# Two instead of three ordinary feature pairs at the head of the second FFN, with token sums and first blocks written out in their order of use

## The chip, the cores and the metric

The kernel runs on one core of one Trainium2 chip. The metric is the device time of one execution in microseconds. The core has a matrix engine (TensorE, PE), a vector engine (VectorE, DVE), a scalar engine (ScalarE, ACT), GpSimd (POOL) and SyncE (SP). Here SyncE issues the plain loads and GpSimd the loads that add to what already lies in on-chip memory.

## The reference

One layer of an encoder on 512 tokens of width 1024, in float32: a half-step SwiGLU FFN, a token-mixing part (two kinds of attention, gated and projected), and a second half-step SwiGLU FFN. Each part stands between two RMS norms.

```python
def _swiglu(x, w_gate, w_up, w_down):
    return (jax.nn.silu(x @ w_gate) * (x @ w_up)) @ w_down
...
f = _swiglu(_rmsnorm(x, ffn2_pre_g[l]), ffn2_w_gate[l], ffn2_w_up[l], ffn2_w_down[l])
x = x + 0.5 * _rmsnorm(f, ffn2_post_g[l])
```

The FFN's inner width is 2816, which the kernel cuts into 22 features of 128. For each feature there is a gate piece and an up piece of weights, each 1024 x 128, stored as 128 partitions x 1024. Gate and up of one feature are called a pair.

## The kernel before

**Precision.** A float32 operand is split in two parts: a rounded one (`hi`, made by ScalarE in line 110) and the remainder (`lo`, made by VectorE in line 111, which must wait for `hi`). Each product of a weight block and tokens is three matmuls, `hi*hi`, `hi*lo` and `lo*hi` (`mm3`, lines 189 to 191).

**Ordinary pairs.** `pair` (line 207) computes one feature the plain way: for gate and for up, eight blocks of 128 rows times 512 tokens, 2 x 8 x 3 = 48 matmuls of 512 columns. The first two pairs of an FFN are made by `first_pairs` (line 216) in two token halves of 256, since the normalised tokens of the second half come later: four projections on the first half, then, after `mid(0)`, four on the second half. After the first two of these pair 0 is finished by `use` and `mid(1)` runs, after the other two pair 1 and `mid(2)`. The first four weight pieces of the second FFN were prepared earlier by DMA (`by_dma`); `fetch` converts two more pieces, if `state["stop"]` still allows it.

**Seven products.** `seven` (line 343) computes a pair with seven instead of eight block products: gate and up on the one side, the two halves of the 1024 rows on the other, and two token halves of 256. It needs sums of weight blocks and sums of token blocks. A pair has the weight blocks 1 to 7: 1 and 2 are the halves of the gate piece (tile `raw`, which has two buffers), 3 is half of the up piece (`w11`), 5 and 7 (`t1`, `t3`) are loaded by SyncE and completed by a load that adds, issued by GpSimd (`load_blocks`, line 319). 6 is 5 + 3 and 4 is 6 + 2, added by VectorE in `sums_of` (line 332), both when block 1 of the pair is made ready. Each block is split into one tile of the tag `w`, which has 12 buffers. The token blocks 1, 2 and 4 are the normalised tokens themselves; 5, 6, 3 and 7 are sums made once for an FFN by the generator `combined` (line 290): its first step adds `hi` and `lo` of the first token half (four additions, line 304), each further step makes one sum (two additions, line 294) and splits it (two splits).

In the loop of `seven`, a turn j multiplies blocks 1, 5, 2, 6 and 3 of pair j and blocks 7 and 4 of pair j-1. Between them the blocks of pair j+1 are made ready, one behind each product, and the loads of pair j+2 are asked for at the top. Each product is 4 x 3 = 12 matmuls of 256 columns, 84 for a pair.

**Order of the work.** The token sums are drawn by `mid` (line 531): two steps in `mid(0)`, two in `mid(1)`, one in `mid(2)`. `STD` (line 35) is 3: three ordinary pairs, the third by `pair` in line 541, then the loop for the other 19 features. Between two marks the instructions of TensorE, ScalarE and VectorE are pinned to the order in which they are written (line 1484). For the second FFN such a stretch ends with `mid(2)`. Behind it, and on SyncE's and GpSimd's queues, a planner in the compiler orders the instructions by what it takes to be ready, with the written order as priority, and it may also put later work between pinned instructions.

The hidden features are kept in an order, `order_of` (line 1539), that the down projection wants. `times` (line 493) multiplies a feature into its place; for the features that ordinary pairs make it keeps the product aside and, once its neighbour is there, GpSimd copies it in (line 508).

Of the kernel before, what the change touches and what calls it, by code (L numbers as in the profile page):

```python
# [16 lines left out]
ALU = mybir.AluOpType  # L17
# [7 lines left out]
NF = 2816 // P  # L25
# [6 lines left out]
SPREAD = 4  # L32
URGENT = 400
FIRST = (4, 5, 6, 7)
STD = 3
BLOCKS = (10, 10)
BYDMA = (2, 3, 4)
AHEAD = 6
WARM = (0, 1, 0, 1, 9, 2)
PINNED = (mybir.EngineType.PE, mybir.EngineType.Activation, mybir.EngineType.DVE)  # L40

# [2 lines left out]
def block_kernel(ctx, tc, x, gains, weights, rpb_near, rpb_all, alibi0, alibi12, out):  # L44
    nc = tc.nc
# [12 lines left out]
    def unit(dt=F32, name="u"):  # L58
        return up.tile([P, 512], dt, tag="u", name=name)
# [49 lines left out]
    def split(hi, lo, src):  # L109
        nc.scalar.copy(hi, src)  # L110
        nc.vector.tensor_tensor(lo, src, hi.bitcast(F32), op=ALU.subtract)  # L111
# [1 line left out]

    pieces = {}
    loads = deque()
    state = {"used": False, "next": 0, "take": 0, "stop": 2 * STD, "ahead": lambda: None}
    ordered = []
    pool = []
    total = weights.shape[0]
# [199 lines left out]
    def load_blocks(n):  # L319


        r = wp.tile([P, PIECE], F32, tag="raw", name="raw", bufs=2)
        w11, t1, t3 = unit(name="w11"), unit(name="t1"), unit(name="t3")
        nc.sync.dma_start(t1, weights[n + 1][:, :512])
        nc.sync.dma_start(t3, weights[n + 1][:, :512])
        nc.sync.dma_start(r, weights[n])
        nc.sync.dma_start(w11, weights[n + 1][:, 512:])
        nc.gpsimd.dma_start(t1, weights[n][:, :512], accum_op=ALU.add)  # L328
        nc.gpsimd.dma_start(t3, weights[n + 1][:, 512:], accum_op=ALU.add)
        return {1: r[:, :512], 2: r[:, 512:], 3: w11, 5: t1, 7: t3}  # L330

    def sums_of(raw):
        t2, t4 = unit(name="t2"), unit(name="t4")
        nc.vector.tensor_tensor(t2, raw[5], raw[3], op=ALU.add)  # L334
        nc.vector.tensor_tensor(t4, t2, raw[2], op=ALU.add)
        raw[6], raw[4] = t2, t4

    def split_block(raw):
        w = wp.tile([P, PIECE], F32R, tag="w", name="w")
        split(w[:, :512], w[:, 512:], raw)  # L340
        return w

    def seven(use, mv, n_pairs, n0, behind, far, lead, raws):

        blocks = {}
        o = {}  # L350

        def get(j):
            if j < n_pairs and j not in raws:
                raws[j] = load_blocks(n0 + 2 * j)
            elif j >= n_pairs:
                behind(far)

        def ready(j, i):
            if j < n_pairs:
                if j and loads:  # L360
                    loads.popleft()()
                if i == 1:
                    sums_of(raws[j])
                blocks[j, i] = split_block(raws[j].pop(i))
            else:
                behind(lead)

        def product(j, i, key, start):
            if start:
                o[key, j] = bank(key)  # L370
            w = blocks.pop((j, i))
            acc = o[key, j][:, :256]
            for k in range(4):
                mm3(acc, w[:, k * P:(k + 1) * P], w[:, 512 + k * P:512 + (k + 1) * P], *mv[i][k],
                    start and k == 0, k == 3, skip_group_check=True)
            return acc

        res = {}
        get(0)
        get(1)  # L380
        for i in (1, 5, 2, 6, 3, 7, 4):
            ready(0, i)
        for j in range(n_pairs + 1):
            now, was = j < n_pairs, j > 0
            get(j + 2)
            if now:
                q = product(j, 1, "q", True)
                g, u = res[j] = unit(name="g"), unit(name="up")
                nc.scalar.copy(g[:, :256], q)
            ready(j + 1, 1)  # L390
            if was:
                q0 = product(j - 1, 7, "q", False)
                g0, u0 = res.pop(j - 1)
                nc.vector.tensor_tensor(u0[:, 256:], u0[:, 256:], q0, op=ALU.subtract)
            ready(j + 1, 5)
            if now:
                p = product(j, 5, "p", True)
                nc.scalar.copy(u[:, 256:], p)
            ready(j + 1, 2)
            if now:  # L400
                r = product(j, 2, "r", True)
                nc.vector.tensor_tensor(g[:, :256], g[:, :256], r, op=ALU.add)
            ready(j + 1, 6)
            if now:
                product(j, 6, "q", False)
                nc.scalar.copy(u[:, :256], q)
            ready(j + 1, 3)
            if was:
                product(j - 1, 4, "q", False)
                use(j - 1, g0, u0, q0)  # L410
            ready(j + 1, 7)
            if now:
                product(j, 3, "p", False)
                nc.vector.tensor_tensor(u[:, :256], p, u[:, :256], op=ALU.subtract)
            ready(j + 1, 4)
# [69 lines left out]
    def ffn(g, store, src):  # L485
        hidden = [None] * NF
        m = BLOCKS[store]
        feats = order_of(m)
        duos = [[None] * m for _ in range(2)]
        parts = {}  # L490
        n0 = state["take"]

        def times(j, a, b):

            k = feats.index(j)
            if k >= 2 * m or j < STD:
                hidden[k] = b
                nc.vector.tensor_tensor(b, a, b, op=ALU.mult)
                return
            to = lambda i, k: duos[i][k // 2][:, (k % 2) * 256:(k % 2) * 256 + 256]  # L500
            parts = [slice(i * 256, i * 256 + 256) for i in range(2)]
            for i, part in enumerate(parts):
                if duos[i][k // 2] is None:
                    duos[i][k // 2] = unit(name="h")
                nc.vector.tensor_tensor(to(i, k), a[:, part], b[:, part], op=ALU.mult)
            if k % 2 and hidden[k - 1] is not None:
                for i, part in enumerate(parts):
                    nc.gpsimd.tensor_copy(to(i, k - 1), hidden[k - 1][:, part])
                hidden[k - 1] = None

        def stat(k):
            if k not in parts:
                parts[k] = unit(F32R), unit(F32R)
                split(*parts[k], hidden[k])
                hidden[k] = None
            return parts[k]

        def use(j, pg, pu):
            h = unit(name="h")
            nc.scalar.activation(h, pg, AF.Silu)  # L520
            times(j, pu, h)

        def use7(j, g, u, q):
            nc.scalar.activation(g[:, :256], g[:, :256], AF.Silu)
            nc.scalar.activation(g[:, 256:], q, AF.Silu)
            times(STD + j, u, g)

        raws = {}
        sums = combined()

        def mid(i):
            if i == 0:
                for j in range(2):
                    raws[j] = load_blocks(n0 + 2 * STD + 2 * j)
            for _ in range((2, 2, 1)[i]):
                next(sums)

        first_pairs(use, (0, 2) if store else (1, 2), mid=mid)
        g_post, g_pre = gain(g), None if store else gain(g + 1)
        for j in range(2, STD):  # L540
            pair(use, j)
        if not store:
            bias_plan()
        after = n0 + 2 * NF
        state["stop"] = total if store else total - 3 * NF - NK

        far, lead, rest = down(m, after, duos, stat, g_post, g_pre, store, src)
        state["next"] = state["take"] = after + 2 * m
        seven(use7, next(sums), NF - STD, n0 + 2 * STD, lambda q: [f() for f in q.popleft()], far, lead, raws)
        rest()  # L550

    def views(raw):
# [127 lines left out]
    def down(m, n0, duos, stat, g_post, g_pre, store, src):  # L680
# [66 lines left out]
        def add_later(i, of, key, wait=0):  # L747
            for d in range(nd):
                later.setdefault(order.index((i, d)) - AHEAD + wait, []).append(ld((key, d), *of(d)))

# [337 lines left out]
    def mixing(g):  # L1088
# [119 lines left out]
        far = [v_far(1), v_far(2)]  # L1208
# [33 lines left out]
        n0 = total - 3 * NF - NK  # L1242
# [3 lines left out]
        sums = []  # L1246
# [31 lines left out]
        ready = []  # L1278
# [15 lines left out]
        for f in range(8):  # L1294
            ya, yb = bank(), bank()
            for k in range(10):
                i, c = divmod((f * 10 + k) * P, PIECE)
# [27 lines left out]
                    rooms.append(o.duo_room("ra", f - 5) if f < 7 else o.duo_room("rb", 0))  # L1325
                    nc.sync.dma_start(rooms[-1], weights[n0 + f])
        state["take"] = state["next"] = n0 + 8
        state["stop"] = total - 3 * NF + 2 * STD

        whole[:] = [[unit(name="whole") for _ in range(2)] for _ in range(2)]  # L1330
        early = [by_dma(n) for n in first_of_next()] * 2
# [48 lines left out]
    raws = []  # L1380
# [5 lines left out]
    for n in range(2, 4):  # L1386
        raw = wp.tile([P, PIECE], F32, tag="raw", name="raw", bufs=2)
# [150 lines left out]

def order_of(m):

    lo = min(STD, NF - 2 * m)
    return [*range(lo, lo + 2 * m), *range(lo), *range(lo + 2 * m, NF)]


# [60 lines left out]
```

## Time and profile before

| | us |
|---|---|
| median of three runs | 1090.49 |
| lowest and highest run | 1090.48, 1091.98 |
| profiled execution | 1090.01 |
| its span | 1088.2 |
| TensorE busy in the span | 1078.8 |
| VectorE busy | 819.7 |
| ScalarE busy | 649.3 |
| GpSimd busy | 177.9 |

Times in the profile's rows count from the start of the span, which is a little shorter than the execution's own time. The second FFN's first projections begin at about 747 us, its seven-product loop at 783.8, its down projection at about 982. Matmuls overlap: a matmul of 256 columns is shown as 0.28 us long, though the next one starts 0.12 us later, so the distance of the starts is what counts. The same holds for VectorE and ScalarE in a queue, where an operation starts before the one ahead of it has fully ended.

### The profile page before, as it was taken

The page shows a single profiled execution, that of the slowest core. Times are in us where ns is not written, and L with a number is a line of the kernel's source. Part 1 is how long each engine was busy: PE and PEld are TensorE (multiplying, and loading weights), DVE is VectorE, ACT ScalarE, POOL GpSimd, SP SyncE. Part 2 cuts the span into 40 slices and gives each one's busy share as a digit, 9 for nine tenths or more (in the row PEclk, how much of TensorE's full clock was granted, in tenths as well). Part 3 has the DMA queues.
Part 4 walks back from the last instruction along what each step waited for, and adds up shares of the span by engine and source line. Part 5 has one row for each costly group of instructions (what it writes and reads, how often), then busy time and mean ns, then how long its engine had stood idle before and what let it go on. Part 6 is the DMA issues. An engine that isn't in the chain of part 4 may idle for free. (4 is left out here: it accounts for less than half of the span.)

```text
span 1088.2 us, 18567 instructions
## 1 busy us (share of the span) xinstructions
PE 1078.8 (99%) x6821; PEld 977.7 (90%) x6821; DVE 819.7 (75%) x1514; ACT 649.3 (60%) x1300; POOL 177.9 (16%) x248
## 2 busy tenths in 40 slices
PE   9999999999999999999999999999999999999997
PEld 7999999998888988888988888888999999998886
DVE  7887777777987679876467654766897777779974
ACT  6555555565584767767656651375565555566662
POOL 3121122012334000000000001133131111114101
PEclk9999999999999999999999999999999999999999
DMA  6899898468994453332232239564577776769932
GB/s 215 223 200 241 217 244 207 138 164 252 233 296 101 126 183 119 135 90 79 66 104 78 78 118 300 162 116 140 140 188 206 196 170 182 200 174 248 237 139 77
DMA packets 90973, 184.59 MB, mean 170 GB/s; under 512 B 23553, under 2 KB 26113, under 8 KB 90882
## 3 DMA queue, kind: packets, MB, share of 16 engines
q1 hardware_dynamic: 64720, 131.03, 35.8%
q0 software_dynamic: 23472, 51.91, 26.8%
q8 instruction: 53, 0.87, 0.3%
q10 hardware_dynamic: 2690, 0.46, 0.2%
q14 instruction: 38, 0.31, 0.1%
HBM read 178.34 MB, written 7.58 MB: 171 GB/s over the span
## 5 line engine op out<-in xcount | busy, mean ns | idle before, releaser
L111 DVE TENSOR_TENSOR w<-raw,w 128x512 fp32r<-128x512 f32 (+1 forms) x139 | 129.3, 931 | 87.6 <-ACT w L110 87.0
L189 PE MATMUL ps<-hn,w 128*128 128x512 f32 (+1 forms) x488 | 174.9, 358 | 0.0
L110 ACT CAST w<-raw 128x512 fp32r<-128x512 f32 (+1 forms) x139 | 113.5, 819 | 102.5 <-DMA raw<-in_weights_dram 41.5
L191 PE MATMUL ps<-hn,w 128*128 128x512 f32 (+1 forms) x488 | 172.4, 353 | 0.0
L190 PE MATMUL ps<-hn,w 128*128 128x512 f32 (+1 forms) x488 | 172.3, 353 | 0.0
L110 ACT CAST w<-t 128x512 fp32r<-128x512 f32 x152 | 93.5, 619 | 52.0 <-DVE t L334 27.9
L111 DVE TENSOR_TENSOR w<-t,w 128x512 fp32r<-128x512 f32 x152 | 103.9, 688 | 27.1 <-ACT w L110 24.4
L191 PEld LDWEIGHTS ps<-hn,w 128*128 128x128 f32 x488 | 92.3, 189 | 12.9
L190 PEld LDWEIGHTS ps<-hn,w 128*128 128x128 f32 x488 | 92.4, 189 | 11.3
L189 PEld LDWEIGHTS ps<-hn,w 128*128 128x128 f32 x488 | 92.4, 189 | 11.3
L189 PE MATMUL q<-v,w 128*128 128x256 f32 x304 | 86.0, 283 | 0.0
L191 PE MATMUL q<-hn,w 128*128 128x256 f32 x304 | 86.0, 283 | 0.0
L189 PE MATMUL p<-v,w 128*128 128x256 f32 x304 | 86.0, 283 | 0.0
L190 PE MATMUL p<-v,w 128*128 128x256 f32 x304 | 86.0, 283 | 0.0
L191 PE MATMUL q<-v,w 128*128 128x256 f32 x304 | 86.0, 283 | 0.0
L190 PE MATMUL q<-v,w 128*128 128x256 f32 x304 | 86.0, 283 | 0.0
L190 PE MATMUL q<-hn,w 128*128 128x256 f32 x304 | 86.0, 283 | 0.0
L189 PE MATMUL q<-hn,w 128*128 128x256 f32 x304 | 86.0, 283 | 0.0
L191 PE MATMUL p<-v,w 128*128 128x256 f32 x304 | 85.9, 283 | 0.0
L328 POOL DMA_DIRECT2D t<-in_weights_dram x38 | 33.3, 877 | 289.5 <-DMA t<-in_weights_dram 67.3
L189 PE MATMUL q<-w,a 128*128 128x512 f32 x176 | 68.5, 390 | 0.0
L190 PE MATMUL q<-w,a 128*128 128x512 f32 x176 | 68.3, 389 | 0.0
(260 smaller groups left out, 2992.6 us busy)
## 6 DMA issues: line engine op xcount, KB each, us to landing
raw<-in_weights_dram SPq DMA_DIRECT2D x103, 512.0 KB
t<-in_weights_dram SPq DMA_DIRECT2D x76, 256.0 KB
t<-in_weights_dram POOLq DMA_DIRECT2D x76, 256.0 KB, 5.3
w<-in_weights_dram SPq DMA_DIRECT2D x38, 256.0 KB
w<-in_weights_dram POOLq DMA_DIRECT2D x36, 256.0 KB, 6.3
rows<-in_weights_dram SPq DMA_DIRECT2D x24, 256.0 KB
tb<-in_weights_dram POOLq DMA_DIRECT2D x12, 512.0 KB, 7.9
x<-in_x_dram SPq DMA_DIRECT2D x16, 256.0 KB
```

The lines of the kernel that those rows point to most:

```text
L110: nc.scalar.copy(hi, src)
L111: nc.vector.tensor_tensor(lo, src, hi.bitcast(F32), op=ALU.subtract)
L189: nc.tensor.matmul(o, sh, mh, start=start, stop=False, **kw)
L190: nc.tensor.matmul(o, sh, ml, start=False, stop=False, **kw)
L191: nc.tensor.matmul(o, sl, mh, start=False, stop=stop, **kw)
L328: nc.gpsimd.dma_start(t1, weights[n][:, :512], accum_op=ALU.add)
```

## The change

In the second FFN alone, `STD` becomes 2: there is no third ordinary pair, and the loop computes 20 features instead of 19. `state["stop"]` follows, so that `fetch` in `first_pairs` converts nothing there. The first FFN keeps three pairs and its order.

The three calls of `mid` now draw the token sums and split the first weight blocks in a written order, `ORDER`. `mid(0)` draws the sums of the halves and then follows its entry, `mid(1)` and `mid(2)` theirs. A `"v"` is the next token sum (5, 6, 3, 7 in turn), a tuple (j, i) is block i of pair j. These instructions lie in the pinned stretch. The sum for block 6 is made just ahead of block 6 and the sum for block 4 just ahead of block 3, in the later pairs too, where the first FFN goes on making both ahead of block 1. The first turn multiplies in the order 1, 2, 5, 6, 3 instead of 1, 5, 2, 6, 3, and block 4 of pair 0 is split after product 6 of that turn.

```diff
-STD = 3
+STD = (3, 2)
...
+ORDER = ("v", (0, 1), (0, 2)), ("v", (0, 5), (0, 6)), ("v", (0, 3), (1, 1), "v", (0, 7))
...
-    def sums_of(raw):
-        t2, t4 = unit(name="t2"), unit(name="t4")
-        nc.vector.tensor_tensor(t2, raw[5], raw[3], op=ALU.add)
-        nc.vector.tensor_tensor(t4, t2, raw[2], op=ALU.add)
-        raw[6], raw[4] = t2, t4
-
-    def split_block(raw):
+    def sum_of(raw, n):
+
+        if n not in raw:
+            raw[n] = unit(name="sum")
+            nc.vector.tensor_tensor(raw[n], *((raw[5], raw[3]) if n == 6 else (raw[6], raw[2])), op=ALU.add)
+
+    def split_block(raw, i):
+        if i in (6, 3):
+            sum_of(raw, {6: 6, 3: 4}[i])
         w = wp.tile([P, PIECE], F32R, tag="w", name="w")
-        split(w[:, :512], w[:, 512:], raw)
+        split(w[:, :512], w[:, 512:], raw[i])
         return w
...
-                if i == 1:
-                    sums_of(raws[j])
-                blocks[j, i] = split_block(raws[j].pop(i))
+                if i == 1 and not early:
+                    sum_of(raws[j], 6)
+                    sum_of(raws[j], 4)
+                if (j, i) not in blocks:
+                    blocks[j, i] = split_block(raws[j], i)
...
-        for i in (1, 5, 2, 6, 3, 7, 4):
+        for i in (1, 2, 5, 6, 3, 7) if early else (1, 5, 2, 6, 3, 7, 4):
             ready(0, i)
+
+        def fifth():
+            p = product(j, 5, "p", True)
+            nc.scalar.copy(u[:, 256:], p)
+            return p
...
-            if now:
-                p = product(j, 5, "p", True)
-                nc.scalar.copy(u[:, 256:], p)
+            if now and (was or not early):
+                p = fifth()
...
             ready(j + 1, 6)
+            if early and not was:
+                p = fifth()
             if now:
                 product(j, 6, "q", False)
                 nc.scalar.copy(u[:, :256], q)
+            if early and not was:
+                ready(0, 4)
...
         def mid(i):
+
             if i == 0:
                 for j in range(2):
-                    raws[j] = load_blocks(n0 + 2 * STD + 2 * j)
-            for _ in range((2, 2, 1)[i]):
+                    raws[j] = load_blocks(n0 + 2 * std + 2 * j)
+            if std > 2:
+                for _ in range((2, 2, 1)[i]):
+                    next(sums)
+                return
+            if i == 0:
                 next(sums)
+            for step in ORDER[i]:
+                if step == "v":
+                    next(sums)
+                else:
+                    blocks[step] = split_block(raws[step[0]], step[1])
...
-        for j in range(2, STD):
+        for j in range(2, std):
             pair(use, j)
...
-        state["stop"] = total - 3 * NF + 2 * STD
+        state["stop"] = total - 3 * NF + 2 * STD[1]
```

More of the change, by code (lines that the diff above doesn't have):

```diff
@@ L115, in block_kernel @@
     loads = deque()
-    state = {"used": False, "next": 0, "take": 0, "stop": 2 * STD, "ahead": lambda: None}
+    state = {"used": False, "next": 0, "take": 0, "stop": 2 * STD[0], "ahead": lambda: None}
     ordered = []
@@ L330, in load_blocks, with seven @@
         return {1: r[:, :512], 2: r[:, 512:], 3: w11, 5: t1, 7: t3}
-    def sums_of(raw):
-        t2, t4 = unit(name="t2"), unit(name="t4")
-        nc.vector.tensor_tensor(t2, raw[5], raw[3], op=ALU.add)
-        nc.vector.tensor_tensor(t4, t2, raw[2], op=ALU.add)
-        raw[6], raw[4] = t2, t4
-    def split_block(raw):
+    def sum_of(raw, n):
[5 more added lines that the diff above has]
+            sum_of(raw, {6: 6, 3: 4}[i])
         w = wp.tile([P, PIECE], F32R, tag="w", name="w")
-        split(w[:, :512], w[:, 512:], raw)
+        split(w[:, :512], w[:, 512:], raw[i])
         return w
-    def seven(use, mv, n_pairs, n0, behind, far, lead, raws):
-        blocks = {}
+    def seven(use, mv, n_pairs, n0, behind, far, lead, raws, blocks):
+        early = bool(blocks)
         o = {}
@@ L370, in product @@
                 o[key, j] = bank(key)
-            w = blocks.pop((j, i))
+            w = blocks[j, i]
             acc = o[key, j][:, :256]
@@ L495, in times @@
             k = feats.index(j)
-            if k >= 2 * m or j < STD:
+            if k >= 2 * m or j < STD[store]:
                 hidden[k] = b
@@ L525, in use7 @@
             nc.scalar.activation(g[:, 256:], q, AF.Silu)
-            times(STD + j, u, g)
-        raws = {}
+            times(STD[store] + j, u, g)
+        raws, blocks = {}, {}
         sums = combined()
+        std = STD[store]
         def mid(i):
@@ L548, in ffn @@
         state["next"] = state["take"] = after + 2 * m
-        seven(use7, next(sums), NF - STD, n0 + 2 * STD, lambda q: [f() for f in q.popleft()], far, lead, raws)
+        seven(use7, next(sums), NF - std, n0 + 2 * std, lambda q: [f() for f in q.popleft()], far, lead, raws, blocks)
         rest()
@@ L1539, in order_of @@
 def order_of(m):
-    lo = min(STD, NF - 2 * m)
+    lo = min(STD[1], NF - 2 * m)
     return [*range(lo, lo + 2 * m), *range(lo), *range(lo + 2 * m, NF)]
```

## The prediction

> **What bounds the kernel now.** I read the page's first part and its chain of waits first: how much of the span is TensorE, and whether anything else stands on the path.
>
> ```profile
> span 1088.2 us, 18567 instructions
> PE 1078.8 (99%) x6821; PEld 977.7 (90%) x6821; DVE 819.7 (75%) x1514; ACT 649.3 (60%) x1300; POOL 177.9 (16%) x248
> ...
> PE 31%; ACT 0%; DVE 0%; POOL 0%; issue 0%; DVEq 0%; POOLq 0%; ACTq 0%
> ```
>
> The chain is TensorE alone, so only two things can move the end: fewer TensorE microseconds, or a new TensorE wait. Next I cut the stage of the change into its steps with the view of windows (columns: stretch, length, busy time and count of PE, PEld, DVE, ACT, POOL, then clock, DMA share, GB/s).
>
> ```profile
> 761.35:772.88 11.53, 11.53 (x98) 11.53 (x97) 7.97 (x12) 4.65 (x8) 1.57 (x2) 1.00 0.91 225
> 772.88:783.79 10.91, 10.91 (x50) 9.02 (x49) 9.68 (x16) 6.71 (x11) 1.75 (x2) 1.00 0.30 48
> 783.79:793.87 10.08, 10.08 (x85) 10.07 (x84) 10.04 (x18) 8.87 (x20) 2.18 (x3) 1.00 0.62 180
> 793.87:803.95 10.08, 10.08 (x86) 10.08 (x86) 10.08 (x20) 5.41 (x13) 4.40 (x4) 1.00 0.78 213
> 870.24:880.32 10.08, 10.08 (x86) 10.08 (x85) 7.72 (x15) 5.75 (x12) 1.76 (x2) 1.00 0.73 181
> 1000.00:1040.00 40.00, 40.00 (x178) 33.12 (x177) 39.03 (x55) 27.55 (x41) 11.64 (x14) 1.00 1.06 249
> ```
>
> The rows are: the second token half of the first two pairs, the third ordinary pair, the first and second period of the seven-product loop, one of its later periods, and a stretch of the down projection. TensorE is full in every one. VectorE is full too in the first two periods of the loop (10.04 and 10.08 of 10.08), and only later falls to 7.72. So VectorE, which prepares what the loop multiplies, is the engine that has no room where the change cuts.
>
> **Part 1: the third pair becomes a twentieth turn of the loop.** The edges of that pair in TensorE's timeline:
>
> ```profile
> 772.76 0.28 PE L191 MATMUL ps<-hn,w 128*128 128x256 f32 x1
> 772.88 0.40 PE L189 MATMUL ps<-hn,w 128*128 128x512 f32 x1
> ...
> 783.57 0.39 PE L191 MATMUL ps<-hn,w 128*128 128x512 f32 x1
> 783.79 0.28 PE L189 MATMUL q<-hn,w 128*128 128x256 f32 x1
> ```
>
> It is 2 projections x 8 blocks x 3 = 48 matmuls of 512 columns from 772.88 to 783.79, 10.91 us or 0.227 each. A loop turn is 7 products x 4 blocks x 3 = 84 matmuls of 256 columns in 10.08 us, 0.120 each. The exchange saves 10.91 - 10.08 = **0.83 us**, and this is all that TensorE can gain: no row shows it waiting elsewhere in the stage. The Trainium skill speaks against the exchange: "TensorE: Matmul & The Clock Gate", section Back-to-back issue gap, gives a sustained spacing in streams of weight load and matmul of about 81 ns at 128 columns and 131 ns at 512. By it, 48 wide ones would take an estimated 6.3 us and 84 of 256 columns no less than 6.8, and the exchange would lose at least 0.5 us. The trace disagrees: this stage's spacing is 227 and 120 ns, so I go by the rows.
>
> **Part 2: what VectorE and ScalarE do at the head.** The cover that goes is the 10.91 us of the third pair: the loop's first product moves from 783.79 to 772.88. VectorE's rows of before, from the last norm on:
>
> ```profile
> 758.88 1.29 DVE L281 TENSOR_TENSOR hn<-ps,hn 128x512 fp32r<-128x512 f32 x2 [1.99 <-ACT hn L280]
> 762.52 2.36 DVE L111 TENSOR_TENSOR w<-raw,w 128x1024 fp32r<-128x1024 f32 x2 [2.35 <-ACT w L110]
> 764.80 2.49 DVE L304 TENSOR_TENSOR sum<-hn 128x512 f32<-128x512 f32 x4
> 767.20 1.29 DVE L294 TENSOR_TENSOR sum<-whole 128x512 f32<-128x512 f32 x2
> ...
> 771.57 0.69 DVE L111 TENSOR_TENSOR w<-raw,w 128x512 fp32r<-128x512 f32 x1 [2.31 <-ACT w L110]
> ...
> 775.04 0.69 DVE L498 TENSOR_TENSOR h<-ps,h 128x512 f32<-128x512 f32 x1 [0.97 <-ACT h L520]
> ...
> 778.23 1.29 DVE L294 TENSOR_TENSOR sum<-sum 128x512 f32<-128x512 f32 x2
> 779.61 1.29 DVE L111 TENSOR_TENSOR v<-sum,v 128x512 fp32r<-128x512 f32 x2
> 780.82 0.68 DVE L498 TENSOR_TENSOR h<-ps,h 128x512 f32<-128x512 f32 x1
> ```
>
> and ScalarE's:
>
> ```profile
> 759.75 1.80 ACT L288 COPY whole<-ps 128x256 f32<-128x256 f32 x6
> 761.33 2.09 ACT L110 CAST w<-raw 128x1024 fp32r<-128x1024 f32 x2
> ...
> 770.92 0.62 ACT L110 CAST w<-raw 128x512 fp32r<-128x512 f32 x1 [2.38 <-DMA raw<-in_weights_dram]
> 771.45 0.62 ACT L110 CAST w<-t 128x512 fp32r<-128x512 f32 x1
> ...
> 773.12 1.28 ACT L520 ACT_TABLE_LOAD   x1
> 774.41 0.60 ACT L520 ACTIVATE h<-ps 128x512 f32<-128x512 f32 x1
> ```
>
> Prices on VectorE: a 512-wide add costs 0.60 in a queue (2.40 for four, 764.80 to 767.20) and its result is there after 0.69; a step of token sums with its two splits 2.59 (778.23 to 780.82, a short wait for ScalarE in it); a block's split 0.60. A block that needs its sum first costs 0.69 + 0.62 (ScalarE's rounding) + 0.60, with the hand-overs 2.0. ScalarE is paced 0.53 (770.92 to 771.45) and has room.
>
> What goes from VectorE: the two 1024-wide splits of the third pair's weights (762.52 to 764.80) with the 2.35 us of idling ahead of them, and one multiplication. What is pinned in instead: blocks 1, 2, 5, 6, 3, 7 of pair 0 and block 1 of pair 1, between the sums. I queue them by these prices from 758.88 + 1.29 = 760.17: the four sums of halves end at 762.6; sums 5 at 765.2 (what they read is there at 759.75 + 1.80 = 761.55); blocks 1 and 2 at 766.4; the first pair's multiplication must wait for the second projection's end (761.35 + 48 x 0.12 = 767.1) and ends at 768.1; sums 6 at 770.7; block 5 at 771.3; block 6 at 773.3; the second multiplication at 773.9; sums 3 at 776.5; the sum for block 4 and block 3 at 777.8; block (1,1) at 778.4; sums 7 at 781.0; block 7 at 781.6.
>
> TensorE wants a product every 12 x 0.12 = 1.44 us from 772.88: product 1 at 772.9, 2 at 774.3, 5 at 775.8, 6 at 777.2, 3 at 778.6, (1,1) at 780.1, 7 at 781.5, (1,5) at 783.0. The margins are about 7, 8, 4.4, 3.8, 0.7, 1.6 and **-0.2 us**; then (1,5) and (1,2) are ready at 782.3 and 782.9 for 783.0 and 784.4. A product's first two matmuls read only the rounded half, which hides most of 0.2. After that a turn asks 7.72 us of VectorE in 10.08 and the queue recovers. I take 0.2 us of stall. Bounds: nothing at the low end, since the work just fits; at the high end one more idle stretch of VectorE as long as the one that before had at 771.57, 2.31 + 0.2 = 2.5 us.
>
> **Part 3: loads.** The pinned splits wait for DMA on ScalarE's queue, and behind a late one stand all later sums, splits and activations, so lateness passes to TensorE almost one to one. SyncE's and GpSimd's queues before, then the wait of SyncE from 740 to 800, and the time to landing from 745 to 800:
>
> ```profile
> 652.74 27.08 SPq L126 DMA_DIRECT2D raw<-in_weights_dram  x5
> ...
> 754.11 0.76 SPq L324 DMA_DIRECT2D t<-in_weights_dram  x1
> ...
> 756.91 0.38 SPq L327 DMA_DIRECT2D w<-in_weights_dram  x1
> 763.77 1.46 SPq L326 DMA_DIRECT2D raw<-in_weights_dram  x2
> ...
> 785.49 0.33 SPq L326 DMA_DIRECT2D raw<-in_weights_dram  x1
> ```
>
> ```profile
> 759.24 0.94 POOL L328 DMA_DIRECT2D t<-in_weights_dram  x1 [4.37 <-PE ps L277]
> ...
> 761.85 1.07 POOL L329 DMA_DIRECT2D t<-in_weights_dram  x1
> ...
> 792.98 4.20 POOL L508 COPY h<-h 128x256 f32<-128x256 f32 x2
> ```
>
> ```profile
> SPq L326 <- DVE w L111: 7.1, 2, 6.4
> ```
>
> ```profile
> t<-in_weights_dram POOLq DMA_DIRECT2D x8, 256.0 KB, 5.6
> ```
>
> Before, pair 0's row block was issued at 763.77, because both of its buffers held the third pair's weights until the split that ended at 764.88 (SyncE's 6.4 us on it), and ScalarE got it at 770.92. The last loads into these buffers had been issued by 679.8, and the change deletes two of them. So I expect the row blocks of pairs 0 and 1 to be issued early, by 757 at the latest beside the other loads; needed is the first at 764.5. The accumulated blocks are issued at 759.24 to 762.9 as before and land 5.6 later, 765 to 768.5; the first is needed at 770.0. I cost both at nothing. The later loads come sooner: pair 2's row block waits for the sum for block 4 (777.2, where before it was issued at 785.49), and its first product is the thirteenth, at 772.88 + 12 x 1.44 = 790.2. A turn more moves more data, but the loop's DMA share is 0.73. GpSimd loses the two copies at 792.98 (4.20 us; what they write is read first in the down projection). In later turns the deferred sums cost the same instructions, under TensorE's 10.08.
>
> **Sum.** The profiled execution took 1090.01 us around its span of 1088.2, 0.48 below the median of 1090.49. By its own time: 1090.01 - 0.83 + 0.2 = 1089.4; on the median: 1090.49 - 0.83 + 0.2 = **1089.9 us**.
>
> **Rivals.**
> 1. *VectorE's line is too dense.* The margins of 0.7 and -0.2 us rest on 0.60 us steps without a break, and unpinned work can slip between. For it: the 2.31 and 0.97 us idle rows. Against it: those idle stretches had causes that the change removes. Price 1 to 2.5 us: 1090.7 to 1092.2, so no visible change.
> 2. *The saving is given back in the down projection*, where VectorE is busy 39.03 of 40.00. Then the end stays at 1090.5. Against it: TensorE is busy 40.00 of 40.00 there, and what VectorE prepares moves with the loop.
> 3. *Slower: a pinned split waits for a late row block.* Place: ScalarE's first split of block 1. If SyncE keeps the block late, so that it lands at 770.92 as before, the line starts 770.92 - 764.5 = 6.4 us late, of which TensorE loses about 6.4 at product 7: 1096.1. It decides for slower when the landing is later than about 767.4. For it: that very wait of 2.38 us stands in the trace. Against it: what held the buffer is gone. The same page of the Trainium skill (What's actually happening) says that an idle window of some 3.4 us halves the clock; no row here shows it.
> 4. *Faster by more than 0.2%*, 2.2 us: nothing in the rows offers TensorE more than 0.83.
>
> **How the numbers follow.** A run of this kernel tells about 0.2% (2.2 us) from no change. Forecast 0.60 (1089.2 to 1090.6), rival 1 0.20, rival 2 0.05, rival 3 0.13, rival 4 0.02. So no change 0.85, slower 0.13, faster 0.02. The range goes from the saving without a stall, less the 0.48 between the profiled execution and the median (1089.2, rounded to 1089.0), to the stall of 2.5 us (1092.2, rounded to 1092.4).
>
> **What would show it.** Right: 48 wide matmuls fewer and 84 narrow ones more; the loop's first product directly behind the last 256-wide projection; TensorE full in the 20 us behind it but for some tenths, at block 7; the row blocks' loads issued before 757. Wrong: an idle row on ScalarE ahead of the split of block 1 that ends with a load, or TensorE gaps over 1 us in that stretch, with VectorE idle beside them (a late load, rival 3) or busy throughout (rival 1).

## The result, and the profile after

| | before, beside it | after |
|---|---|---|
| median of the runs, us | 1090.90 | 1093.96 |
| lowest and highest, us | 1089.94, 1093.62 | 1092.10, 1095.57 |
| profiled execution, us | 1090.01 | 1094.09 |

The ratio after to before is 1.0026, with a 95% interval of 1.0018 to 1.0035: the change makes the kernel 0.26% (2.8 us) slower; the two medians lie 3.06 us apart. All ratios here are of fast runs alone, and one run is left out by that, a single execution of e9 below that took 5516 us. The forecast was 1089.9 us, and 1093.96 lies above its range. On the page of after, the first part and the chain of waits:

```profile
span 1092.3 us, 18647 instructions
...
PE 1081.2 (99%) x6857; PEld 981.4 (90%) x6857; DVE 820.4 (75%) x1525; ACT 647.5 (59%) x1309; POOL 175.2 (16%) x248
...
PE 29%; DVE 1%; ACT 1%; issue 0%; POOL 0%; DVEq 0%; POOLq 0%; ACTq 0%
```

Two things stand in it. The chain, TensorE alone before, now has a hundredth each of VectorE and ScalarE. And TensorE is busy 2.4 us longer (1081.2 against 1078.8), although the exchange of the third pair for a turn should have saved 0.8. The view of windows on the same stage (columns as in the prediction) tells where:

```profile
761.97:773.50 11.53, 11.53 (x99) 11.53 (x97) 9.61 (x17) 7.04 (x12) 1.74 (x2) 1.00 0.55 92
773.50:777.82 4.32, 4.32 (x39) 4.32 (x37) 4.24 (x8) 2.43 (x5) 0.00 (x0) 1.00 0.00 0
777.82:782.77 4.95, 2.77 (x18) 2.16 (x17) 4.86 (x9) 3.26 (x8) 0.29 (x1) 0.98 0.74 234
782.77:785.34 2.57, 2.57 (x13) 2.57 (x13) 2.57 (x6) 2.57 (x7) 1.43 (x2) 0.50 1.05 363
785.34:790.66 5.32, 5.32 (x44) 5.32 (x44) 5.22 (x10) 2.94 (x8) 1.75 (x2) 0.94 0.94 201
790.66:800.98 10.32, 10.32 (x88) 10.32 (x87) 8.71 (x17) 6.34 (x14) 1.76 (x2) 1.00 0.96 246
```

The first row is the second token half of the first pairs, as long as before (11.53). Then products 1, 2 and 5 of pair 0 run at full rate. In the third row TensorE is busy 2.77 of 4.95 us. In the fourth it is busy throughout, but the granted clock is 0.50. So there are two losses: waiting, and a slow clock behind it. TensorE's timeline resolves both (in brackets: idle before the matmul, and what ended it):

```profile
777.94 0.28 PE L191 MATMUL q<-hn,w 128*128 128x256 f32 x1
778.93 0.39 PE L192 MATMUL q<-hn,w 128*128 128x256 f32 x1 [0.71 <-DVE w L112]
...
780.10 0.28 PE L192 MATMUL q<-hn,w 128*128 128x256 f32 x1
781.82 0.38 PE L190 MATMUL p<-v,w 128*128 128x256 f32 x1 [1.45 <-ACT w L111]
...
782.34 0.42 PE L190 MATMUL r<-hn,w 128*128 128x256 f32 x1
...
782.77 0.42 PE L190 MATMUL q<-v,w 128*128 128x256 f32 x1
...
785.98 0.28 PE L190 MATMUL p<-v,w 128*128 128x256 f32 x1
786.10 0.28 PE L191 MATMUL p<-v,w 128*128 128x256 f32 x1
```

The tiles tell the products apart: `q<-hn` from 777.82 is product 1 of *pair 1*, `p<-v` at 781.82 and `r<-hn` at 782.34 are the first two matmuls each of products 5 and 2 of pair 1, and `q<-v` at 782.77 is **product 6 of pair 0**, which in the written order stands directly behind product 5 of pair 0 and was wanted at 777.82. It comes 4.95 us late; the planner filled the time with what it had of pair 1, and TensorE still waits 0.99 - 0.12 = 0.87 and 1.72 - 0.12 = 1.60 us. From 782.77 to 785.98 fifteen matmuls start 0.214 apart instead of 0.120, and at 785.98 the full rate is back.

What product 6 reads was there. It needs block 6, in VectorE's timeline of after the first of these rows:

```profile
773.20 0.69 DVE L112 TENSOR_TENSOR w<-sum,w 128x512 fp32r<-128x512 f32 x1 [0.69 <-ACT w L111]
...
778.19 0.68 DVE L112 TENSOR_TENSOR w<-raw,w 128x512 fp32r<-128x512 f32 x1
...
781.38 0.69 DVE L112 TENSOR_TENSOR w<-t,w 128x512 fp32r<-128x512 f32 x1
```

Block 6 is ready at 773.89, block (1,1) at 778.87, block 7 at 782.07. What product 6 did not have was its *bank*. It is called with `start` False: it adds onto bank `q`, in which product 1 stands, and so may not begin before ScalarE has copied product 1 out (`nc.scalar.copy(g[:, :256], q)`, L400 after the change). ScalarE's timeline of after:

```profile
776.77 0.61 ACT L111 CAST w<-raw 128x512 fp32r<-128x512 f32 x1
779.51 1.22 ACT L111 CAST v<-sum 128x512 fp32r<-128x512 f32 x2 [2.12 <-DVE sum L295]
780.64 1.13 ACT L111 CAST w<-t 128x512 fp32r<-128x512 f32 x2
781.68 0.61 ACT L111 CAST w<-raw 128x512 fp32r<-128x512 f32 x1
782.20 0.36 ACT L400 COPY g<-q 128x256 f32<-128x256 f32 x1
782.46 0.37 ACT L391 COPY up<-p 128x256 f32<-128x256 f32 x1
```

Product 1's last matmul ends at about 775.1, but its copy runs at 782.20. Ahead of it on ScalarE stand the last roundings that `mid(2)` pins (block 3, block (1,1), token sums 7, block 7) and the planner's next ones, and ScalarE idles 2.12 us at 779.51 for token sums 7 with the copy behind it in the queue. The copy ends at 782.20 + 0.36 = 782.56, and product 6 starts at 782.77.

The loads, in SyncE's timeline of after:

```profile
673.92 7.29 SPq L327 DMA_DIRECT2D raw<-in_weights_dram  x2
...
777.73 0.33 SPq L327 DMA_DIRECT2D raw<-in_weights_dram  x1
778.11 0.42 SPq L325 DMA_DIRECT2D t<-in_weights_dram  x1
```

The row blocks of pairs 0 and 1 are issued a hundred microseconds ahead.

**The accounting.** The beginning of the kernel varies between executions, so I measure from the start of the work behind the first two pairs (772.88 before, 773.50 after) to the start of the last matmul, and take from TensorE's timeline of each kernel by how much the distances of starts exceed the usual ones: over 0.13 us of excess counts as waiting, less as slow starts. There is one profiled execution of each kernel.

| profiled execution | stretch, us | against before | waiting | slow starts |
|---|---|---|---|---|
| before | 308.38 | | 0 | 0 |
| after | 311.94 | +3.56 | 2.65 | 1.80 |

For after, -0.83 + 2.65 + 1.80 = 3.62, against 3.56 measured. Most of the slow starts are the half clock: the granted clock is 0.50 from 782.57 to 785.98, and the sixteen matmuls that start in these 3.41 us take 1.49 us more than 16 x 0.12. The rest are single starts beside a wait, which lie some 0.22 us apart in e1 too, where the granted clock is 1.00. With the 0.62 of the later beginning this makes 4.18, and the profiled executions are 1094.09 - 1090.01 = 4.08 apart.

### The profile page after: what moved, and what is told of

Its sections match the earlier page's. It is cut to its first block, busy times and chain, and to the rows that moved or that the text cites. A ratio compares the mean times of both kernels' runs of the same rounds, so it can differ in the third digit from the quotient of the medians.

```text
span 1092.3 us, 18647 instructions
## 1 busy us (share of the span) xinstructions
PE 1081.2 (99%) x6857; PEld 981.4 (90%) x6857; DVE 820.4 (75%) x1525; ACT 647.5 (59%) x1309; POOL 175.2 (16%) x248
## 5 line engine op out<-in xcount | busy, mean ns | idle before, releaser
L190 PE MATMUL ps<-hn,w 128*128 128x512 f32 (+1 forms) x472 | 168.6, 357 | 0.0
L192 PE MATMUL ps<-hn,w 128*128 128x512 f32 (+1 forms) x472 | 166.1, 352 | 0.0
L191 PE MATMUL ps<-hn,w 128*128 128x512 f32 (+1 forms) x472 | 166.1, 352 | 0.0
L192 PEld LDWEIGHTS ps<-hn,w 128*128 128x128 f32 x472 | 89.3, 189 | 12.2
L191 PEld LDWEIGHTS ps<-hn,w 128*128 128x128 f32 x472 | 89.4, 190 | 10.7
L190 PEld LDWEIGHTS ps<-hn,w 128*128 128x128 f32 x472 | 89.3, 189 | 10.7
L190 PE MATMUL p<-v,w 128*128 128x256 f32 x312 | 88.6, 284 | 1.4 <-ACT w L111 1.4
L192 PE MATMUL q<-hn,w 128*128 128x256 f32 x312 | 88.4, 283 | 0.7 <-DVE w L112 0.7
L191 PE MATMUL q<-v,w 128*128 128x256 f32 x312 | 88.8, 285 | 0.0
L192 PE MATMUL q<-v,w 128*128 128x256 f32 x312 | 88.8, 285 | 0.0
L190 PE MATMUL q<-v,w 128*128 128x256 f32 x312 | 88.8, 285 | 0.0
L191 PE MATMUL p<-v,w 128*128 128x256 f32 x312 | 88.5, 284 | 0.0
L191 PE MATMUL q<-hn,w 128*128 128x256 f32 x312 | 88.3, 283 | 0.0
L190 PE MATMUL q<-hn,w 128*128 128x256 f32 x312 | 88.3, 283 | 0.0
L192 PE MATMUL p<-v,w 128*128 128x256 f32 x312 | 88.1, 283 | 0.0
L190 PE MATMUL q<-w,a 128*128 128x512 f32 x176 | 68.5, 390 | 0.0
L191 PE MATMUL q<-w,a 128*128 128x512 f32 x176 | 68.3, 389 | 0.0
L192 PE MATMUL q<-w,a 128*128 128x512 f32 x176 | 68.0, 389 | 0.0
L111 ACT CAST w<-sum 128x512 fp32r<-128x512 f32 x78 | 48.3, 621 | 28.6 <-DVE sum L337 22.5
```

Of the source, the lines that this page charges most:

```text
L190: nc.tensor.matmul(o, sh, mh, start=start, stop=False, **kw)
L191: nc.tensor.matmul(o, sh, ml, start=False, stop=False, **kw)
L192: nc.tensor.matmul(o, sl, mh, start=False, stop=stop, **kw)
```

## The experiments

**Theory A**: product 6 waits for the copy of product 1, which stands behind ScalarE's pinned line. The first rival is the prediction's rival 1: VectorE's line is too dense, and what TensorE waits for is blocks (the names in its brackets above, `w` of VectorE and ScalarE, speak for this one). A third view gives the clock the main part, and a fourth, Theory C of the expectations, the planner's order of the products. Line numbers are each kernel's own; where an edit moves lines, the operation and the tiles tell which it is.

| kernel | median, us | before beside it | ratio and interval | stretch against before | waiting | slow starts |
|---|---|---|---|---|---|---|
| e1 copies first | 1090.59 | 1091.03 | 0.9995 (0.9986 to 1.0004) | -0.14 | 0.44 | 0.31 |
| e2 TensorE as written | 1096.42 | 1091.03 | 1.0044 (1.0031 to 1.0056) | +5.31 | 5.05 | 1.12 |
| e3 clock kept | 1093.08 | 1091.03 | 1.0015 (1.0006 to 1.0024) | +2.09 | 0 | 0.07 |
| e4 two pairs, old order | 1095.03 | 1091.03 | 1.0033 (1.0021 to 1.0044) | +3.83 | 3.23 | 1.49 |
| e5 three pairs, new order | 1091.62 | 1091.29 | 1.0004 (0.9996 to 1.0013) | -0.06 | 0 | 0 |
| e6 sum 4 later | 1091.89 | 1091.29 | 1.0001 (0.9992 to 1.0010) | +0.44 | 1.23 | 0.10 |
| e8 block 7 first | 1090.85 | 1091.29 | 0.9998 (0.9989 to 1.0007) | +0.07 | 0.86 | 0.10 |
| e9 first turn written | 1089.99 | 1091.12 | 0.9989 (0.9981 to 0.9998) | -0.80 | 0 | 0.09 |
| e10 and product 1 of pair 1 | 1091.07 | 1091.12 | 0.9993 (0.9985 to 1.0002) | -0.89 | 0 | 0 |

In every kernel with two pairs the stretch against before is -0.83 plus waiting plus slow starts, within about 0.1 us; in e3 the added matmuls come on top.

### e1: the copies ahead of the last pinned roundings

The first turn's products 1, 2 and 5 with their copies are written, and pinned, ahead of token sums 7 and block 7.

```diff
-ORDER = ("v", (0, 1), (0, 2)), ("v", (0, 5), (0, 6)), ("v", (0, 3), (1, 1), "v", (0, 7))
+ORDER = ("v", (0, 1), (0, 2)), ("v", (0, 5), (0, 6)), ("v", (0, 3), (1, 1))
...
+            if early and not was:
+                r = product(j, 2, "r", True)
+                nc.vector.tensor_tensor(g[:, :256], g[:, :256], r, op=ALU.add)
+                p = fifth()
+                tail()
+                ordered[-1][1] = mark()
...
+        def tail():
+            next(sums)
+            blocks[0, 7] = split_block(raws[0], 7)
+            next(sums)
```

> The token sums 7 and block 7 of pair 0 are drawn behind the products 1, 2 and 5 of the first turn and ScalarE's two copies of their results, and the pinned stretch reaches to there; all else as in the changed kernel. Theory A: product 6 adds onto the bank of product 1, so it must wait until ScalarE has copied product 1's result, and that copy stands behind every pinned split. Then the copy runs at about 777.5 instead of 782.2, product 6 follows product 5 with no gap over 0.3 us, the half-speed stretch is gone, and the time is the kernel before less 0.8: ratio to before 0.9990 to 1.0000. Theory B: VectorE is too dense, and TensorE waits for blocks. Then the gaps move but stay over 1.5 us in sum, and the ratio stays above 1.0015. Theory C: the planner's order of the products (product 1 of pair 1 ahead of product 6 of pair 0) is the cause by itself. Then the ratio depends on its new order alone, and gaps come wherever it puts a product of pair 1 first.

The two copies in ScalarE's timeline of e1, and TensorE in its windows from the loop's start:

```profile
776.74 0.36 ACT L400 COPY g<-q 128x256 f32<-128x256 f32 x1
777.47 0.37 ACT L391 COPY up<-p 128x256 f32<-128x256 f32 x1 [0.37 <-PE p L192]
```

```profile
772.95:781.47 8.52, 8.52 (x73) 8.52 (x72) 8.21 (x15) 5.81 (x13) 0.00 (x0) 1.00 0.35 108
781.47:784.26 2.79, 2.51 (x20) 2.16 (x18) 2.79 (x6) 2.58 (x6) 1.51 (x2) 1.00 0.54 167
```

Counted from the loop's start, the copy of product 1 comes (782.20 - 773.50) - (776.74 - 772.95) = 4.9 us sooner, product 6 starts at 777.51 without a gap, behind two matmuls of pair 1, and the 4.45 us of waiting and slow starts shrink to 0.75, though VectorE is nearly as busy (8.21 of 8.52 us, against 8.35 in as long a stretch of after). What is left is product 7's wait for the remainder of block 7 (VectorE), which ends at 782.96. So A holds the main part of the loss, and rival 1 some 0.4 us.

### e2: TensorE alone held to the written order

```diff
+        start = mark()
         get(0)
...
+            if early and j == 1:
+                pool.append((start, mark(), (mybir.EngineType.PE,)))
```

> TensorE alone is held to the written order of the products through the first two turns; ScalarE and VectorE are as in the changed kernel. Theory A: product 6 now stands directly behind product 5 and waits for the copy at about 782.6 with nothing to fill the wait: one idle stretch of some 4.5 us from 777.8, and the time is 0 to 3 us above the changed kernel, ratio to before 1.003 to 1.006. Theory B: product 6's data is ready at about 774, so it starts at 777.8 and the gap comes later, ahead of block 7 or block 5 of pair 1; ratio about 1.002. Theory C: the gaps go, ratio 0.9990 to 1.0005.

If blocks were what is late, the written order would cost little: the blocks are made in that order. If it is the copy, product 6 waits openly. The waits of e2, its copy on ScalarE, and its windows:

```profile
PE q L190 <- ACT g L401: 4.6, 1, 4.6
```

```profile
782.90 0.36 ACT L401 COPY g<-q 128x256 f32<-128x256 f32 x1
```

```profile
778.41:783.32 4.91, 0.28 (x4) 0.08 (x2) 4.82 (x9) 3.10 (x7) 0.12 (x1) 0.96 0.72 233
783.32:786.26 2.94, 2.94 (x14) 2.94 (x15) 2.94 (x7) 2.94 (x7) 1.59 (x2) 0.50 1.06 351
```

One wait of 4.6 us, of `q` for the copy to `g`, between the last matmul of product 5 at 778.41 and product 6 at 783.32. In after the planner's filling hides this wait, and shows in its place the blocks of pair 1 for which the filling itself waits. So the planner's order isn't the cause (Theory C): kept to the written order, the stretch is +5.31 instead of +3.56, and the filling had won back 1.75 us.

### e3: TensorE kept busy while it waits

Behind product 5 of the first turn 24 matmuls go into a bank that nothing reads; the rest is as in after.

```diff
                 p = fifth()
+                junk = bank("junk")
+                for k in range(24):
+                    nc.tensor.matmul(junk[:, :256], blocks[0, 1][:, k % 4 * P:(k % 4 + 1) * P], mv[1][k % 4][0], start=True, stop=True)
```

> 24 matmuls of 256 columns into an unused bank are put behind product 5 of the first turn, 2.9 us at 0.12 each; their result is not read. They fill what was idle, so that the clock gate sees no idle stretch; product 6 can start no earlier. If the half-speed stretch from 781.8 to 785.9 (about 20 matmuls at 0.214 instead of 0.120, 1.9 us) comes from the idling, it goes, and the time falls by 1.5 to 1.9 us against the changed kernel: ratio to before 1.0008 to 1.0015. If it has another cause, the time stays or grows: 1.0026 and more.

The added matmuls in TensorE's timeline, and the window behind them:

```profile
777.79 3.04 PE L418 MATMUL junk<-hn,w 128*128 128x256 f32 x24
```

```profile
782.66:786.77 4.11, 4.11 (x37) 4.11 (x36) 4.11 (x8) 4.11 (x10) 2.23 (x4) 1.00 1.10 315
```

They start over 24 x 0.12 = 2.88 us, which takes the place of 2.65 us of waiting, and the clock stays at 1.00 behind them. The stretch is +2.09 against -0.83 + 2.88 = 2.05 worked out. So the slow clock is a consequence of TensorE's idling here. In the medians, each against before beside it, e3 gains 0.11% on after, near the 3.56 - 2.09 = 1.47 us (0.13%) that the stretch gives; the two intervals overlap, so the size stands on the profiled executions.

### e4 and e5: one part of the change alone

e4 has two pairs with the old order of `mid`, e5 the new order with three pairs.

```diff
 e4
-            if std > 2:
+            if True:
 e5
-STD = (3, 2)
+STD = (3, 3)
...
-            if std > 2:
+            if not store:
```

> Two ordinary pairs, but the old order: the token sums alone are pinned (two steps, two, one), the blocks are made ready in the loop, sums for blocks 6 and 4 ahead of block 1, products 1, 5, 2, 6, 3. Theory A: the pinned line of ScalarE is shorter by seven splits, but the copy of product 1 still stands behind the last token sums, and the blocks come behind them: gaps of 2 to 5 us, ratio 1.002 to 1.005. Theory B: VectorE has the same work in a worse order, ratio 1.003 and more. If the written order is what costs, the ratio is 0.999 to 1.000.

> The other half of the change alone: three ordinary pairs as before, but the blocks pinned between the token sums and the first turn in the new order. Theory A: the copy of product 1 again stands behind the last pinned splits, but these end at about 783 and the third pair covers TensorE until 784, so there is nothing to wait for: ratio 0.9995 to 1.0005, no TensorE gap over 0.3 us. If the new order costs by itself, as in a late row block or a denser VectorE, the ratio is over 1.001.

The wait of e4 that answers to the second gap of after, and its copy of product 1; then the third pair and the first turn in e5's windows:

```profile
PE q L190 <- ACT w L111: 2.5, 1, 2.5
```

```profile
781.98 0.36 ACT L400 COPY g<-q 128x256 f32<-128x256 f32 x1
```

```profile
774.52:785.43 10.91, 10.91 (x50) 9.03 (x49) 9.54 (x16) 5.59 (x10) 0.00 (x0) 1.00 0.00 0
785.43:795.51 10.08, 10.08 (x86) 10.07 (x85) 9.99 (x18) 7.78 (x17) 3.67 (x5) 1.00 0.86 268
```

The loss comes with the missing pair alone: with three pairs the new order costs nothing and brings nothing, because the third pair's 10.91 us lie between the pinned line and the first product. With two pairs the old order loses 0.33%, the new one 0.26%, with overlapping intervals: that the new order takes a part of the loss away isn't shown. In e4 too the copy runs at 782. That wait of 2.5 us ends with a block's rounding, so in e4 alone A and rival 1 can't be told apart.

### e6 and e8: the rest of e1, by moving VectorE's work

e6 is e1 with the sum for block 4 of pair 0 made ahead of block 4 instead of block 3, which takes 0.6 us from VectorE ahead of block 7. e8 is e6 with block 7 split ahead of token sums 7.

```diff
 e6, against e1
-        if i in (6, 3):
-            sum_of(raw, {6: 6, 3: 4}[i])
+        if i in (6, 4) or i == 3 and not late:
+            sum_of(raw, {6: 6, 3: 4, 4: 4}[i])
...
 e8, against e6
         def tail():
-            next(sums)
             blocks[0, 7] = split_block(raws[0], 7)
             next(sums)
+            next(sums)
```

> The kernel with the copies ahead of token sums 7, and one addition of VectorE (the sum for block 4 of pair 0) moved from ahead of block 3 to ahead of block 4, behind the pinned stretch. In the kernel with the copies first, some 0.9 us of gaps were left at block 7 of pair 0 (781.6 to 783.2), where VectorE had run without idling. If these are VectorE's density, 0.60 us less ahead of block 7 shortens them to 0.2 to 0.4 us, and the time falls by some 0.5 us: ratio to before 0.9988 to 0.9995. If they have another cause, the gaps stay at 0.9 us and the ratio at 0.9995.

> As the kernel with the sum for block 4 later, and block 7 of pair 0 split ahead of token sums 7 instead of behind them, so that VectorE splits it while ScalarE rounds. Block 7 is then ready some 2 us earlier and the token sums 7 at about 781.5, when TensorE wants them. If VectorE's order is all that is left, no TensorE gap over 0.2 us remains, the saving of 0.83 us is there in full, and the ratio to before is 0.9988 to 0.9995; otherwise gaps of 0.5 us and more stay in the first two turns.

VectorE's timeline of e6 just ahead of block 7, whose remainder is in the last row:

```profile
781.61 0.42 DVE L432 TENSOR_TENSOR up<-p,up 128x256 f32<-128x256 f32 x1 [0.57 <-PE p L192]
...
782.55 0.69 DVE L337 TENSOR_TENSOR sum<-t,w 128x512 f32<-128x512 f32 x1
783.15 0.69 DVE L337 TENSOR_TENSOR sum<-sum,raw 128x512 f32<-128x512 f32 x1
783.75 1.29 DVE L112 TENSOR_TENSOR w<-t,w 128x512 fp32r<-128x512 f32 x2
```

e6 missed: the planner put unpinned work into the freed room, a subtraction that idles 0.57 us for TensorE and two sums of weight blocks, and the waiting grew from 0.44 to 1.23 us. e8 missed as well: that wait is gone, and another one shows, in the waits and in ScalarE's timeline:

```profile
PE q L190 <- ACT g L400: 0.7, 1, 0.7
```

```profile
789.29 0.36 ACT L400 COPY g<-q 128x256 f32<-128x256 f32 x1
```

This is A again, one turn on: product 6 of pair 1 adds onto the bank of product 1 of pair 1, whose copy is late at 789.29. Nothing is pinned there: the copy stands behind roundings that the planner put ahead of it, one of which idles 2.65 us for a sum of VectorE. So what delays a copy is its place in ScalarE's queue, pinned or not.

### e9 and e10: the whole first turn written out

e9 pins the first turn as the dependencies ask for it: each copy directly behind its product, and a block or sum as late as its product allows.

```diff
+                r = product(j, 2, "r", True)
+                nc.vector.tensor_tensor(g[:, :256], g[:, :256], r, op=ALU.add)
+                p = fifth()
+                blocks[0, 7] = split_block(raws[0], 7)
+                product(j, 6, "q", False)
+                nc.scalar.copy(u[:, :256], q)
+                tail()
+                product(j, 3, "p", False)
+                nc.vector.tensor_tensor(u[:, :256], p, u[:, :256], op=ALU.subtract)
+                ready(1, 5)
+                ready(1, 2)
+                ordered[-1][1] = mark()
...
```

Here `tail` makes token sums 7 alone. e10 pins product 1 of pair 1 with its copy and product 7 of pair 0 as well:

```diff
                 ready(1, 2)
+                first(1)
+                seventh(1)
                 ordered[-1][1] = mark()
...
```

> The whole first turn is written out and pinned: products 1, 2, 5, then block 7, product 6 and the copy of its result, token sums 7, product 3, and blocks 5 and 2 of pair 1; the sum for block 4 stays early. Theory A with VectorE as the next limit: product 6 waits 0.2 us at most, block 7 and token sums 7 are ready when TensorE wants them, and from the end of the first pairs to the last matmul it takes 307.6 to 308.0 us, against 308.38 before and 308.24 in the kernel with the copies first. The ratio is 0.9988 to 1.0000, which five rounds hardly tell from no change. If VectorE is short of time whatever the order, gaps of 0.5 us and more stay, and that stretch takes 308.2 or more.

> As the kernel with the first turn written out, and product 1 of pair 1, the copy of its result and product 7 of pair 0 pinned behind it, ahead of the blocks 6, 4, 3, 7 that follow: the same cure for the next product 6, which must wait for that copy. Theory A: no wait for a copy is left in the second turn either, 307.6 to 307.9 us from the end of the first pairs to the last matmul, ratio 0.9988 to 0.9998. If the planner had placed the copy well without it, there is no difference to the kernel with the first turn alone.

The copies in ScalarE's timeline of e9 (product 1, 5 and 6 of pair 0), and its first two turns in the windows:

```profile
777.41 0.36 ACT L400 COPY g<-q 128x256 f32<-128x256 f32 x1
778.13 0.37 ACT L391 COPY up<-p 128x256 f32<-128x256 f32 x1 [0.36 <-PE p L192]
...
779.81 0.37 ACT L408 COPY up<-q 128x256 f32<-128x256 f32 x1
```

```profile
773.61:783.69 10.08, 10.08 (x86) 10.08 (x85) 9.85 (x18) 6.75 (x15) 0.88 (x2) 1.00 0.40 130
783.69:793.77 10.08, 10.08 (x86) 10.05 (x85) 10.08 (x19) 9.26 (x20) 2.02 (x3) 1.00 0.74 190
```

TensorE is full in both turns, with VectorE at 9.85 and 10.08 of 10.08: dense as it is, its line holds. The stretch is 0.80 us shorter than before in e9 and 0.89 in e10, the 0.83 of the exchange. By the medians e9 is 1.1 us under before (0.11%, inside the 0.2% that I take as the mark). It is the only one of the nine whose interval lies below no change, and of nine intervals of 95% one can do so by luck, so the gain on before stands on the stretch; on after the gain is clear of both intervals. e10 has the same gain in the stretch and can't be told from before in total. In e9 the copy of product 1 of pair 1 runs at 785.62 without holding TensorE up, so the pinning of e10 had next to nothing left to cure.

## Why the prediction was wrong, point by point

**Part 1 held.** The exchange is worth 0.83 us, but only where nothing waits: -0.80 and -0.89 in e9 and e10, and it is in the sum of every other kernel with two pairs.

**Part 2 is where it failed: the margin of product 6.** "About 7, 8, 4.4, 3.8" priced the time at which its *block* is ready, and that part held: 773.3 was worked out for block 6, 778.4 for (1,1) and 781.6 for block 7, and 773.89, 778.87 and 782.07 were measured, on a beginning 0.62 later. Product 6 has a second condition, which the queue of Part 2 left out, the copy of product 1. That ScalarE "has room" was true of its time (3.26 of 4.95 us busy in the stretch) and said nothing of its order: the copy stands behind block 7's rounding. With the prediction's own steps that rounding is done at 781.6 - 0.69 = 780.9, the copy at 780.9 + 0.36 = 781.3, and product 6, wanted at 777.2, waits **4.1 us** instead of having 3.8 to spare. Where TensorE keeps the written order it waited 4.6 (e2). The bound of 2.5 us was too small for the same reason: it came from VectorE alone.

The profile of before had shown it, in rows that I did not quote. TensorE's timeline of before, then ScalarE's:

```profile
788.10 0.28 PE L189 MATMUL q<-hn,w 128*128 128x256 f32 x1
...
788.74 0.28 PE L190 MATMUL r<-hn,w 128*128 128x256 f32 x1
788.86 0.31 PE L189 MATMUL q<-v,w 128*128 128x256 f32 x1
```

```profile
788.37 0.36 ACT L389 COPY g<-q 128x256 f32<-128x256 f32 x1
```

Product 6 begins at 788.86, right behind the copy's end at 788.73, and six matmuls of pair 1 are slipped in just ahead. There the copy stood behind roundings too, but the third pair had put the pinned line 10.91 us ahead: product 6 came 0.76 us after 788.10, when it was wanted, and those six matmuls filled the time. The cover that Part 2 named as removed had covered this copy too.

**The clock was no term of the sum.** The slow starts made 1.80 of the 4.45 us lost, 1.49 of it at half clock. A stall was priced at its own length; here the waiting drew a slow stretch behind it (e3). The prediction names the half clock beside rival 3 alone, without a price.

**Part 3 held for the row blocks** (those of pairs 0 and 1 issued at 673.92, where 757 was the latest expected, that of pair 2 at 777.73, where 777.2 was worked out) and was wrong on the `t` blocks of pair 2. They come later and not sooner, the first at 778.11 where before issued it at 765.88, and they stand on SyncE's queue behind the row block that waits for its buffer. TensorE did not wait for it in after. In e8 the row block of pair 2, whose buffer the later sum frees later, is issued at 787.24, and ScalarE waits 0.99 us for it; TensorE's one wait there is the copy's.

**The rivals.** Rival 1 (VectorE too dense) is real but small: 0.44 us of waiting in e1, at block 7, and e9 shows VectorE's line holding at 9.85 of 10.08. Rival 2 did not happen: in e9 and e10 the stretch to the last matmul keeps the 0.8 us. Rival 3 had the sign and the engine (a queue in order on ScalarE, with something late at its head), but the wrong place and price: the loads were early, and what ScalarE's line waited for was token sums 7. The row named as the sign against the forecast, TensorE gaps over 1 us with VectorE busy throughout, did appear and would have been read as rival 1; it took e1 and e2 to put it to the copy.

**Open.** The medians of e9 and e10 differ by 1.1 us with nearly equal stretches. In the two profiled executions, 2.23 us apart, the difference lies ahead of the loop: the loops of the second FFN start at 773.61 and 775.94, and those of the first FFN, which both kernels write alike, already at 46.86 and 48.50. Whether this holds for the medians isn't shown. Why the planner doesn't put the copy into ScalarE's 2.12 us of idling ahead of token sums 7 was not tried.

## What to carry to other kernels

A product's margin is the least of *all* that its first matmul waits for: the operands, and the bank it adds to or reuses, with the queue in which the engine that empties the bank stands. When a stretch that covers a written order is taken out, go through the order engine by engine and look for unpinned instructions that the next product needs and that queue behind pinned ones. And the tile named at the end of a wait may only be that of the filling: hold the stalled engine to its written order, and the wait that matters stands alone.

## What the runs showed of the hardware

The granted clock falls after less idling than I had thought of. In after TensorE is busy 1.85 of the 4.00 us from 777.82 to 781.82 and idle in two gaps, and from 782.57 to 785.98 the clock is 0.50 and the starts lie at about 0.214 us instead of 0.120. The rows of windows of after give the length of the half clock: 0.02 x 4.95 / 0.50 + 2.57 + 0.06 x 5.32 / 0.50 = 3.41 us. In e2 the 4.91 us gap with next to no work (0.28 busy) has a half clock behind it for 2.94 us, and the 0.96 in the gap's row puts another 0.4 us into the gap. Waits of 0.44 to 1.23 us in sum (e1, e6, e8) left the clock at 1.00. The Trainium skill ("TensorE: Matmul & The Clock Gate", What's actually happening) has the clock at half speed after at least one idle window of about 3.4 us. e2 agrees with it; in after no stretch of that length was free of matmuls, and the clock fell all the same, so by this trace a window that is only partly idle can do.

The beginning of the kernel, up to the end of the second FFN's first two pairs, took 772.9 to 775.9 us in the profiled executions. A difference under 3 us between two of them is better read from a stretch with fixed ends than from the span.
